# A hybrid attention / linear-attention layer: the low-rank gate projection taken from the scaled tokens, its shift added as a bias

## The chip, the cores and the metric

The kernel runs on one core of one Trainium2 chip. A core has five engines that run side by side, each with its own queue of instructions in order: TensorE (PE in the profile; its weight loads are listed apart as PEld), VectorE (DVE), ScalarE (ACT), GpSimd (POOL) and SyncE (SP), which here only issues transfers. Matrix products accumulate in PSUM, a small memory of banks of 128 partitions by 512 fp32 numbers; everything else lies in SBUF. The metric is the device time of one execution in microseconds (us); the kernel before took 1984.97 us as the median of three runs (1984.95 to 1985.31).

## The reference, cut to what matters

The layer works on 256 latent tokens and 256 context tokens of width 2048, in fp32. The change touches one small projection of it, the low rank of the decay gates of the linear attention (GLA):

```python
h  = rms_norm(x, g_mix) * (1 + scale) + shift          # scale, shift: one vector each for latent, one each for context
qa, ka, va, qb, kb, vb, rb, lrf, lrb, gate_a, gate_b = split(h @ w_in)
gf = log_sigmoid(lrf @ w_gate_f + b_gate_f) / 16       # lrf, lrb: 16 columns each of h @ w_in
gb = log_sigmoid(lrb @ w_gate_b + b_gate_b) / 16
```

`lrf` and `lrb` are together 32 of the 13344 columns of `w_in`. The scale and shift vectors come from a product of the conditioning vector with `w_mod` (2048 by 12288). All that follows (two token mixers, the merge, the feed-forward part) is untouched.

## The kernel before, in words

**Tiles.** Tokens are held transposed: 2048 features as 16 K tiles of 128 partitions, by 256 tokens. The input tokens stand in four buffers `xr0` to `xr3` (`xr0`, `xr1`: latent, K tiles 0 to 7 and 8 to 15; `xr2`, `xr3`: context), 8 KB in each partition. They are 4 of the 16 slots of the tag "M". The products with the large weights are made in a split form: an fp32 number is the sum of a rounded part (`hi`) and a rest (`lo`), both in the type fp32r, and a product is three passes, hi·hi, lo·hi, hi·lo. The split tokens `h00hi`, `h00lo`, ... (first digit latent or context, second digit the half of the K tiles) take 8 more M slots. Weights come in blocks of 512 KB (`raw`, 7 slots), and ACT and DVE split them into `whi` and `wlo` (L207, L208; 3 slots each). A plain fp32 product, without the split, appears in the trace as two records.

**The opening.** The scale and shift vectors are not there at the start, so the first stage goes through the 16 K tiles in five groups (0-1, 2-3, 4-7, 8-11, 12-15). For each group `mod_both` loads the columns of `w_mod` (tile `mraw`, 1 MB each, M slots), multiplies them on PE (`pm`, L95), turns the result (`mtr`, DVE L324) into columns (`pcol`, PE L95, then copies L334), and then `affine_scale` (L488) multiplies the tokens by scale and norm factor **in place in `xr`**, and `affine_shift` (L495, L496) adds the shift and writes `hi` and `lo`. With these the group's K tiles of four blocks of projections run: QB twice, KB, VB (`acc`, L83), added up over the groups in SBUF (L505). The modulation products of the next group are put between the projection's products (`tick`, `midway`, `mid`), so PE does them while the loads of the weights go on. Every load of this stage goes through `load`, which fixes their order on SP's queue; a load that waits for a slot holds up all behind it. In the groups up to 8-11 the order of PE's products is fixed by hand (`opening`, `pe_seq`); after that the scheduler of the language orders them by its own cost model, by position in the program first. A slot of a tag is given to the next tile when the last reader of the old one is done.

**The low rank.** After the last group (L656 to L680) the 32 columns of `w_in` are fetched by POOL's queue into `wlr` (pieces of 128 bytes), and 64 plain fp32 products make the low rank: for 4 K tiles at a time, for latent and context, for `hi` and for `lo`, four products into four quarters of 32 partitions of one bank `pl` (L665; tile name `plr` in the trace). ACT copies the bank to `lrp` (L670), four products with a selection matrix add the four quarters and spread the sum to all of them (L673), and ACT and DVE form the split left factor `lr` (tile `wgl`, L676, L679). Then `gla_A` starts: its first product is `pz` (L705, in the trace L95), which needs `lr`. Beside it, PE runs the second KB block (`kb_block`, L855), whose products are free of the low rank.

**PSUM.** `bank` gives out banks of two tags, "main" (1 bank) and "side" (3 banks). `pm` is a side bank; `pcol` is a main bank; so are `plr` and `plr2`. The tag "fb" has 4 buffers and holds, in this stage, `cS` (the conditioning vector, to the last modulation product), the `mtr`, `wlr` and `lrp`.

Of the kernel before, what the change touches and what calls it, by code (L numbers as in the profile page):

```python
# [8 lines left out]
F32 = mybir.dt.float32  # L9
F32R = mybir.dt.float32r  # L10
U8 = mybir.dt.uint8
AF = mybir.ActivationFunctionType
# [4 lines left out]
P = 128  # L17
D = 2048
T = 256
KT = D // P  # L20
# [5 lines left out]
LR, GA, GB = 9216, 9248, 11296  # L26
# [5 lines left out]
def layer_kernel(ctx, tc, A, out):  # L32
    nc = tc.nc
    V, S, G, PE = nc.vector, nc.scalar, nc.gpsimd, nc.tensor
# [12 lines left out]
    w_in = A["w_in"][0]  # L47
    F2_BUFS = {"fa": 4, "fb": 4, "fc": 6}

    def M(name, shape, dt=F32):  # L50
        return big.tile(shape, dt, name=name, tag="M")

    def W2(tag, name, shape, dt=F32):
        return f2.tile(shape, dt, name=name, tag=tag, bufs=F2_BUFS[tag])

    def bank(name, shape=(P, 512), side=False):

        return ps.tile(list(shape), F32, name=name, tag="side" if side else "main", bufs=3 if side else 1)
# [11 lines left out]
    last, pin = [None], [None]  # L70

    opening = []

    def pe_seq(i):

        if opening and opening[0] is not i.ins:
            in_order(opening[0], i.ins)
            opening[:] = [i.ins]
        return i
# [14 lines left out]
    def mm_b(*a, **k):  # L94
        return pe_seq(after(PE.matmul(*a, **k)))  # L95
# [6 lines left out]
    def load(dst, src):  # L102

        d = nc.sync.dma_start(dst, src).ins
        last_load[:] = [d]
        if chain and chain[-1] is None:
            chain[:] = [d]
        elif chain:
            tc.add_manual_dep(d, chain[-1].name, mybir.DependencyInfo(
                mybir.DependencyClass.NoSync, mybir.DependencyReason.DATA), reason="order of loads")  # L110
            chain[:] = [d]
        return d
# [8 lines left out]
    xr = [M(f"xr{i}", [P, 8, T]) for i in range(4)]  # L121
# [96 lines left out]
    def proj_nat(w, r0, c0, kts, lhs, evac, by_tile=False, mid=None):  # L218


        banks = [acc.tile([P, 512], F32, name="acc", tag="acc") for _ in lhs]
        mms = []
        for k0 in kts[::2]:
            tick()
            nk = min(2, kts[-1] + 1 - k0)
            hi, lo = wsplit(w[r0 + k0 * P:r0 + (k0 + nk) * P, c0:c0 + 512])

            def part0(i):
                for k in range(nk):
                    kt = k0 + k  # L230
                    ahi, alo = lhs[i](kt)
                    mm(banks[i], ahi, hi[:, k, :], start=(kt == kts[0]), stop=False)
                    mms.append(mm(banks[i], alo, hi[:, k, :], start=False, stop=False).ins)

            def part1(i):
                for k in range(nk):
                    kt = k0 + k
                    mms.append(mm(banks[i], lhs[i](kt)[0], lo[:, k, :], start=False,
                                         stop=(kt == kts[-1])).ins)

            if by_tile and k0 + nk > kts[-1]:
                for i in range(len(lhs)):
                    if i == len(lhs) // 2:
                        midway()
                    part0(i)
                    part1(i)
                    if i:
                        in_order(end, mms[-4])
                    end = mms[-1]
            else:  # L250
                for part in (part0, part1):
                    for i in range(len(lhs)):
                        part(i)
                    if part is part0:
                        (mid or midway)()
        for i in range(len(lhs)):
            evac(i, banks[i])
# [46 lines left out]
    ALL = list(range(KT))  # L304


    def mod_both(part, t0, n, dst, put=None):

        a = []
        w = n * P  # L310
        nk = 16 // n

        def step(k0):
            if k0 == 0:
                a.append(bank(f"pm{part}_{t0}", (P, w), side=True))
            raw = M("mraw", [P, nk, w])
            load(raw, A["w_mod01"][part, t0 + k0 // nk].rearrange("p (c d) -> p c d", c=nk))
            for k in range(nk):
                kt = k0 + k
                q = 32 * (kt % 4)  # L320
                mm_b(a[0][q:q + 32, :], cS[:, kt, :], raw[:, k, :], start=(kt < 4), stop=(kt >= 12))
            if k0 == KT - nk:
                tr = W2("fb", "mtr", [P, n, 4, 32])
                V.transpose(tr.rearrange("p a b c -> p (a b c)"), a[0])  # L324
                a.append(tr)
                if put is not None:
                    put(end)

        def end():
            pc = bank(f"pcol{part}_{t0}", (32, n * 4, 2))  # L330
            mm_b(pc, sel[:, 0:32], a[1].rearrange("p a b c -> p (a b) c")[:, :, 0:2], start=True, stop=True)
            pv = pc.rearrange("p (a b) c -> p b c a", b=4)
            for b4 in range(4):
                V.tensor_copy(dst[32 * b4:32 * b4 + 32, :, t0:t0 + n], pv[:, b4, :, :])  # L334
            b0 = part * 16 + t0
            d = dst[:, :, t0:t0 + n]
            V.tensor_tensor(d, d, bmod[:, b0:b0 + n].unsqueeze(1).to_broadcast([P, 2, n]), op=ALU.add)

        steps = [lambda k0=k0: step(k0) for k0 in range(0, KT, nk)]
        return steps if put is not None else steps + [end]  # L340
# [48 lines left out]
    shift1 = cst.tile([P, 2, KT], F32, name="shift1")  # L389
# [110 lines left out]
    def add_to(dst, first):  # L500
        def evac(i, b):
            if first:
                S.activation(dst(i), b, AF.Copy)
            else:
                V.tensor_tensor(dst(i), dst(i), b, op=ALU.add)  # L505
        return evac

    hh, hl = [[], []], [[], []]
# [34 lines left out]
    kts = ALL[0:2]  # L543
# [36 lines left out]
    hold.extend([None, i])  # L580
    hold_hi.extend([None, j])

    for gi, (t0, n) in enumerate(groups):
        if gi == 0:
            continue
        kts = ALL[t0:t0 + n]
        flush()
        while bg_steps:
            bg_steps.pop(0)()
        flush()  # L590
        mid = None
        if gi + 1 < len(groups):
            bg_steps.extend(mods[gi + 1][0] + mods[gi + 1][1])
            ticks = 4 * ((n + 1) // 2)
            bg_rate[:] = [1.4 * len(bg_steps) / ticks + 0.01, 0.0]
            if gi == 1:
                bg_rate[:] = [0.0, 0.0]
                steps = iter([1, 2, 1, 2, 2, 0])

                def mid():  # L600
                    pin[0] = last[0]
                    for _ in range(next(steps)):
                        bg_steps.pop(0)()
                    pin[0] = None
        if t0 == 8:
            more_h(1)
        for s in range(2):
            if gi > 1:
                affine_scale(s, t0, n)
                affine_shift(s, t0, n)  # L610
            if s == 0:
                for j in range(2):
                    if j and mid is not None:
                        mid()
                    proj_T(w_in, QB + j * 512, kts, [h_all(0)], add_to(lambda i, j=j: qb0[2 * j + i], False),
                           mid=mid if j else None)
                if mid is not None:
                    mid()
        proj_T(w_in, KB, kts, [h_all(0), h_all(1)], add_to(lambda i: kbt[:, i, :], False), mid=mid)
        if mid is not None:  # L620
            mid()
        proj_nat(w_in, 0, VB, kts, h_xc, add_to(lambda i: vb0[:, i, :], False), mid=mid)
        if gi > 2:
            opening.clear()

# [3 lines left out]
    gate = cst.tile([P, 2], F32, name="gate")  # L629
# [23 lines left out]
    V.tensor_tensor(wg[64:P, :], wtm[64:P, :], wg[64:P, :].bitcast(F32), op=ALU.subtract)  # L653


    wlr = W2("fb", "wlr", [P, KT, 32])  # L656
    G.dma_start(wlr, w_in[:, LR:LR + 32].rearrange("(k p) d -> p k d", p=P))
    behind_gate.__exit__(None, None, None)
    pl = bank("plr")
    for k4 in range(4):  # L660
        for s in range(2):
            for part in (hh, hl):
                for k in range(4):
                    kt = 4 * k4 + k
                    PE.matmul(pl[32 * k:32 * k + 32, s * T:(s + 1) * T], wlr[:, kt, :],  # L665
                              part[s][kt // 8][:, kt % 8, :].bitcast(F32),
                              start=(k4 == 0 and s == 0 and part is hh),
                              stop=(k4 == 3 and part is hl), skip_group_check=True)
    lrp = W2("fb", "lrp", [P, 512])
    S.activation(lrp, pl, AF.Copy)  # L670
    pl = bank("plr2")
    for j in range(4):
        PE.matmul(pl[32 * j:32 * j + 32, :], sel[:, 0:32], lrp, start=True, stop=True)  # L673
# [500 lines left out]
    for half, blocks in enumerate((range(0, 6), range(6, 11))):  # L1174
        n = len(blocks)
# [128 lines left out]
```

## Time and profile before

| | us |
|---|---|
| median of 3 runs | 1984.97 |
| the profiled execution's own time | 1985.05 |
| its span, first to last instruction | 1983.1 |
| PE busy in the span | 1958.6 |
| DVE busy | 1400.0 |
| ACT busy | 971.2 |
| the 64 low-rank products, from the first's start to the next product of PE | 201.43 to 208.47 |

The page of the profile lists busy times and groups of instructions; the view of stretches gives busy time, granted clock and DMA traffic of chosen windows; the timeline lists instructions in order of time, merged, with "start us, us, engine line op out<-in shapes xcount [idle before <-releaser]"; the view of waits sums the idle time of an engine by what ended it. Times in the timeline count from the start of the span. The duration of a PE record includes its way through the array, so what a product costs is read from the distance of starts.

### The profile page before, as it was taken

How to read it: one execution, taken by the hardware profiler on the slowest of the kernel's cores; microseconds unless marked ns; L12 is line 12 of the kernel's file. 1: busy time of each engine (PE TensorE's matmuls, PEld its weight loads, DVE VectorE, ACT ScalarE, POOL GpSimd, SP SyncE). 2: the span in 40 equal slices, each digit the busy share in tenths (PEclk: the TensorE clock that was granted, in tenths of full speed). 3: DMA queues.
4: the chain of work that ended last, by engine and by line, in shares of the span. 5: the costliest groups of instructions: out<-in, count | busy, mean ns of one | idle time of the engine just before them, and what ended most of it. 6: DMA issues, size and time to landing. Idle time of an engine off the chain costs nothing.

```text
span 1983.1 us, 27131 instructions
## 1 busy us (share of the span) xinstructions
PE 1958.6 (99%) x10324; PEld 1637.9 (83%) x10324; DVE 1400.0 (71%) x2150; ACT 971.2 (49%) x1413; POOL 44.5 (2%) x61
## 2 busy tenths in 40 slices
PE   7999999999999999999999999999999999999999
PEld 5679888888887788888888888888888888888887
DVE  5765667876858888777776457889887555677754
ACT  4323555553345666444444445755555334555532
POOL 0010010112000000000000000000000000000000
PEclk9999999999999999999999999999999999999999
DMA  9965222336753456888888668688886566666563
GB/s 379 413 262 178 65 85 75 107 98 196 249 156 112 127 181 210 267 289 287 295 281 272 232 224 282 193 271 278 259 275 232 192 193 190 190 190 184 190 215 113
DMA packets 183603, 420.90 MB, mean 212 GB/s; under 512 B 12544, under 2 KB 12768, under 8 KB 178736
## 3 DMA queue, kind: packets, MB, share of 16 engines
q1 hardware_dynamic: 181856, 413.19, 63.8%
q0 software_dynamic: 1440, 5.80, 1.0%
q8 instruction: 81, 1.33, 0.3%
q14 instruction: 50, 0.41, 0.1%
q10 hardware_dynamic: 176, 0.17, 0.0%
HBM read 416.98 MB, written 2.13 MB: 211 GB/s over the span
## 4 chain that ended last, share of the span: by engine, by line
PE 68%; DVE 0%; ACT 0%; issue 0%; DVEq 0%
PE acc L83 52%; PE accs L83 12%; PE poa L95 1%; PE pS L95 1%; PE ptp L98 1%; PE pto L98 0%; PE ptx L98 0%; DVE wlo L208 0%; ACT s L973 0%; PE ptq L98 0%; DVE s L978 0%; DVE yd L1225 0%; DVE yd L1219 0%; DVE raw L365 0%; ACT whi L207 0%
## 5 line engine op out<-in xcount | busy, mean ns | idle before, releaser
L208 DVE TENSOR_TENSOR wlo<-raw,whi 128x1024 fp32r<-128x1024 f32 x568 | 694.8, 1225 | 435.0 <-ACT whi L207 394.7
L207 ACT ACTIVATE whi<-raw 128x1024 fp32r<-128x1024 f32 x568 | 601.1, 1059 | 773.3 <-PE acc L83 619.4
L83 PE MATMUL accs<-h,whi 128*128 128x512 f32 x704 | 176.3, 392 | 0.0
L83 PE MATMUL acc<-h,whi 128*128 128x512 f32 x640 | 160.4, 392 | 0.0
L83 PEld LDWEIGHTS accs<-h,whi 128*128 128x128 f32 x704 | 126.6, 189 | 22.6
L83 PE MATMUL acc<-whi,h01hi 128*128 128x512 f32 x352 | 139.9, 398 | 0.0
L83 PE MATMUL acc<-whi,h00hi 128*128 128x512 f32 x352 | 139.0, 395 | 0.0
L83 PE MATMUL acc<-whi,h00lo 128*128 128x512 f32 x352 | 138.0, 392 | 0.0
L83 PE MATMUL acc<-whi,h01lo 128*128 128x512 f32 x352 | 137.9, 392 | 0.0
L83 PE MATMUL acc<-whi,al 128*128 128x512 f32 x352 | 137.0, 389 | 0.0
L83 PE MATMUL acc<-whi,ah 128*128 128x512 f32 x352 | 137.0, 389 | 0.0
L83 PEld LDWEIGHTS acc<-h,whi 128*128 128x128 f32 x640 | 115.1, 189 | 20.6
L83 PEld LDWEIGHTS accs<-h,wlo 128*128 128x128 f32 x704 | 96.0, 190 | 6.8
L83 PE MATMUL acc<-wlo,h01hi 128*128 128x512 f32 x352 | 98.7, 396 | 0.0
L83 PE MATMUL accs<-h,wlo 128*128 128x256 f32 x704 | 98.2, 282 | 0.0
L83 PE MATMUL acc<-wlo,h00hi 128*128 128x512 f32 x352 | 97.7, 394 | 0.0
L83 PE MATMUL acc<-wlo,ah 128*128 128x512 f32 x352 | 94.3, 389 | 0.0
L83 PEld LDWEIGHTS acc<-h,wlo 128*128 128x128 f32 x640 | 87.4, 190 | 6.3
L83 PE MATMUL acc<-h,wlo 128*128 128x256 f32 x640 | 89.4, 282 | 0.0
L365 DVE CUSTOM_DVE_ANT_0 raw<-raw,csrow,pack 128x1024 f32<-128x1024 f32 x64 | 81.7, 1284 | 0.0
L83 PEld LDWEIGHTS acc<-whi,ah 128*128 128x128 f32 x352 | 66.1, 188 | 13.7
L83 PEld LDWEIGHTS acc<-whi,al 128*128 128x128 f32 x352 | 66.1, 188 | 13.6
(389 smaller groups left out, 3566.0 us busy)
## 6 DMA issues: line engine op xcount, KB each, us to landing
raw<-in_w_in SPq DMA_DIRECT2D x208, 512.0 KB, 4.4
raw<-in_w_up SPq DMA_DIRECT2D x176, 512.0 KB, 3.9
raw<-in_w_modT SPq DMA_DIRECT2D x128, 512.0 KB, 4.6
raw<-in_w_down SPq DMA_DIRECT2D x88, 512.0 KB, 3.7
mraw<-in_w_mod SPq DMA_DIRECT2D x32, 1024.0 KB, 13.3
raw<-in_w_attn_o SPq DMA_DIRECT2D x32, 512.0 KB, 4.9
raw<-in_w_gla_o SPq DMA_DIRECT2D x32, 512.0 KB, 4.7
raw<-in_w_out SPq DMA_DIRECT2D x32, 512.0 KB, 4.8
```

What stands on the lines that cost most here:

```text
L83: r = pe_seq(PE.matmul(*a, **k))
L95: return pe_seq(after(PE.matmul(*a, **k)))
L98: return pe_seq(after(PE.transpose(*a)))
L207: j = S.activation(hi[:, 0:n, :], raw[:, 0:n, :], AF.Copy).ins
L208: i = V.tensor_tensor(lo[:, 0:n, :], raw[:, 0:n, :], hi[:, 0:n, :].bitcast(F32), op=ALU.subtract).ins
L365: i0 = V.tensor_tensor_reduce(out=raws[i], in0=raws[i], in1=row[0], scale=1.0, scalar=d if h else bmod[:, b0:b0 + 1], op0=ALU.mult, op1=AL ...
```

## The change

The low rank is made from the scaled tokens in `xr` before the shift is added. Since h = xs + shift, the low rank of h is that of xs plus the low rank of the shift, which is one number for each of the 32 columns, for latent and for context. So the products run over `xr` (fp32, one part in place of `hi` and `lo`): 32 in place of 64, eight K tiles at a time, in two runs; the first stands behind the VB products of the group 4-7, the second behind those of the group 12-15. Both add into one bank `pl`, of the tag main, which is held from the first run to the end of the second. `pcol` moves to the tag side. The shift's share is made by 16 products with two moving columns (latent, context) into a bank `plb`; ACT copies it to two columns (into the old tile `gate`) and adds them as a bias while it copies `pl` to `lrp`, in two instructions of 256 columns in place of one of 512. `wlr` is now loaded on SP's queue, in the fixed order of loads, behind the weights of the second group, from a host array `k_wlr` that holds the 32 columns with 2 KB in a row for each partition; the load on POOL's queue goes.

```diff
         def end():
-            pc = bank(f"pcol{part}_{t0}", (32, n * 4, 2))
+            pc = bank(f"pcol{part}_{t0}", (32, n * 4, 2), side=True)
...
     hold_hi.extend([None, j])
 
+    wlr = W2("fb", "wlr", [P, KT, 32])
+    load(wlr.rearrange("p k d -> p (k d)"), A["k_wlr"])
+    pl = bank("plr")
+
+    def low_rank(kts):
+        for k4 in kts[::4]:
+            for s in range(2):
+                for kt in range(k4, k4 + 4):
+                    q = 32 * (kt % 4)
+                    pe_seq(PE.matmul(pl[q:q + 32, s * T:(s + 1) * T], wlr[:, kt, :],
+                                     xr[2 * s + kt // 8][:, kt % 8, :], start=(k4 == 0 and s == 0),
+                                     stop=(k4 == 12), skip_group_check=True))
+
...
         proj_nat(w_in, 0, VB, kts, h_xc, add_to(lambda i: vb0[:, i, :], False), mid=mid)
+        if t0 == 4:
+            low_rank(range(0, 8))
+        if t0 == 12:
+            opening[:] = [last[0]]
+            low_rank(range(8, KT))
         if gi > 2:
             opening.clear()
...
-    wlr = W2("fb", "wlr", [P, KT, 32])
-    G.dma_start(wlr, w_in[:, LR:LR + 32].rearrange("(k p) d -> p k d", p=P))
     behind_gate.__exit__(None, None, None)
-    pl = bank("plr")
-    for k4 in range(4):
-        for s in range(2):
-            for part in (hh, hl):
-                for k in range(4):
-                    kt = 4 * k4 + k
-                    PE.matmul(pl[32 * k:32 * k + 32, s * T:(s + 1) * T], wlr[:, kt, :],
-                              part[s][kt // 8][:, kt % 8, :].bitcast(F32),
-                              start=(k4 == 0 and s == 0 and part is hh),
-                              stop=(k4 == 3 and part is hl), skip_group_check=True)
+    pb = bank("plb", (P, 2), side=True)
+    for kt in ALL:
+        q = 32 * (kt % 4)
+        PE.matmul(pb[q:q + 32, :], wlr[:, kt, :], shift1[:, :, kt], start=(kt < 4), stop=(kt >= 12))
+    pbs = gate
+    S.activation(pbs, pb, AF.Copy)
     lrp = W2("fb", "lrp", [P, 512])
-    S.activation(lrp, pl, AF.Copy)
+    for s in range(2):
+        S.activation(lrp[:, s * T:(s + 1) * T], pl[:, s * T:(s + 1) * T], AF.Identity, bias=pbs[:, s:s + 1])
```

More of the change, by code (lines that the diff above doesn't have):

```diff
@@ L1292 @@
     data["w_upT"] = data["w_up"][0, :, 0:512].T.reshape(4, P, 2, 1024).transpose(0, 2, 1, 3)
+    data["k_wlr"] = data["w_in"][0, :, LR:LR + 32].reshape(KT, P, 32).transpose(1, 0, 2).reshape(P, KT * 32)
     data.update(consts)
```

## The prediction

> **What bounds the kernel now.** I read the page first, then the stretches of the opening, then PE's waits, then the timeline around the low rank.
>
> ```profile
> span 1983.1 us, 27131 instructions
> PE 1958.6 (99%) x10324; PEld 1637.9 (83%) x10324; DVE 1400.0 (71%) x2150; ACT 971.2 (49%) x1413; POOL 44.5 (2%) x61
> PE 68%; DVE 0%; ACT 0%; issue 0%; DVEq 0%
> ```
>
> PE is busy 99% of the span, and the chain that ended last is PE's own work. A busy record alone does not prove a full engine, so the stretches follow: window, length, then busy time of PE, PEld, DVE, ACT and POOL, granted clock, DMA share, GB/s.
>
> ```profile
> 0.00:36.00 36.00, 26.96 (x190) 20.48 (x191) 19.62 (x41) 18.37 (x25) 1.38 (x6) 0.95 0.97 369
> 36.00:101.00 65.00, 61.28 (x478) 42.82 (x477) 44.74 (x103) 21.10 (x34) 0.00 (x0) 1.00 1.02 412
> 101.00:201.40 100.40, 99.49 (x686) 84.66 (x684) 58.60 (x99) 30.86 (x41) 7.34 (x13) 1.00 0.64 215
> 201.40:208.50 7.10, 7.10 (x130) 4.09 (x129) 2.39 (x4) 0.00 (x0) 0.00 (x0) 1.00 0.25 74
> 208.50:1983.10 1774.60, 1763.72 (x8851) 1485.86 (x8847) 1274.62 (x1907) 900.91 (x1314) 35.82 (x42) 1.00 0.63 202
> ```
>
> Up to 36 us PE is held by loads. From 36 to 101 the DMA engines are full (share 1.02, 412 GB/s) and PE is 94% busy (61.28 of 65). From 101 on PE hardly stops, and for the 7.1 us of the low rank it does nothing else. What PE waits for between 36 and 201.4 is all in four rows:
>
> ```profile
> PE pcol L95 <- DVE mtr L324: 2.6, 4, 0.8
> PE acc L83 <- DVE wlo L208: 1.1, 3, 0.6
> PE acc L83 <- ACT h10hi L495: 0.7, 1, 0.7
> PE acc L83 <- DVE h10lo L496: 0.2, 1, 0.2
> ```
>
> No row names a transfer. So a microsecond taken from PE behind 36 us should reach the end, as long as no new wait takes its place.
>
> **The change part by part.** The stage it shortens:
>
> ```profile
> 201.43 0.64 PE L665 MATMUL plr<-h00hi,wlr 128*32 128x256 f32 x8
> 201.88 0.61 PE L665 MATMUL plr<-h00lo,wlr 128*32 128x256 f32 x8
> 207.93 0.61 PE L665 MATMUL plr<-h11lo,wlr 128*32 128x256 f32 x8
> 208.47 0.39 PE L83 MATMUL acc<-h00hi,whi 128*128 128x256 f32 x1
> 208.61 0.60 ACT L670 ACTIVATE lrp<-plr 128x512 f32<-128x512 f32 x1 [7.82 <-PE plr L665]
> 209.38 1.07 PE L673 MATMUL plr<-lrp,pack 128*32 128x512 f32 x8
> 210.51 0.69 ACT L676 ACTIVATE wgl<-plr,pack 128x512 fp32r<-128x512 f32 x1 [1.30 <-PE plr L673]
> 211.23 1.52 DVE L679 SCALAR_TENSOR_TENSOR wgl<-plr,pack,wgl 32x512 fp32r<-32x512 f32 x2 [7.44 <-ACT wgl L676]
> 213.59 0.63 PE L95 MATMUL pz<-wgl 128*128 128x512 f32 x2
> ```
>
> Removed: 64 products in 16 rounds of four (eight records each). The first starts at 201.43, the next product of PE at 208.47: **-7.04 us**.
>
> Added, the two runs: 32 products of the same shape, eight rounds. From the first to the last of the 16 rounds is 207.93 - 201.43 = 6.50 over 15, so 0.433 a round: **+3.46 us**, half at the end of the group 4-7, half in the old place. The first run stands between VB products and a modulation product of its own shape, so it changes the array's shape no oftener than before.
>
> Added, the two-column products: 16, so 32 records, 128 by 32 weights, two moving columns. None so narrow is in the trace. Nearest rows:
>
> ```profile
> 203.18 0.13 PEld L665 LDWEIGHTS plr<-h00hi,wlr 128*32 128x32 f32 x4
> 209.38 0.16 PEld L673 LDWEIGHTS plr<-lrp,pack 128*32 128x32 f32 x8
> 41.57 0.20 PE L95 MATMUL pcol<-mtr,pack 128*32 128x16 f32 x1 [0.57 <-DVE mtr L324]
> 41.63 0.18 PE L95 MATMUL pcol<-mtr,pack 128*32 128x16 f32 x1
> ```
>
> Four loads into four column groups are over in 0.13, eight in 0.16; so 32 take 8 x 0.13 = 1.04 or 4 x 0.16 = 0.64. Two records with 16 columns into one column group start 0.06 apart, which makes 32 x 0.06 = 1.9. A gain is excluded: they are new work on a full engine. I take **+1.04**, since the products go round the four groups as in the first row; ends 0.64 and 1.9.
>
> Added on ACT, behind these products: the copy of two columns, and two copies of 256 columns for one of 512. A copy of 512 took 0.60 (208.61); the shortest ends are nothing and one more such copy, so the chain to `pz` grows by 0 to 0.6. What hides it is the KB block on PE. In the trace `lr` for the first direction is done at 211.23 + 1.52 = 212.75 and `pz` starts at 213.59, 0.84 of slack. A chain 0.6 longer just fits. **+0.1**, ends 0 and 0.6. Queued behind the longer wait on ACT are `whi` copies for later KB products, three slots of which were filled before.
>
> Moved: `wlr` goes onto SP's queue at about 34 us. At 412 GB/s its 256 KB take 0.62 us, and every later load lands so much later. A block of that stage:
>
> ```profile
> 81.63 1.06 ACT L207 ACTIVATE whi<-raw 128x1024 fp32r<-128x1024 f32 x1 [1.96 <-DMA raw<-in_w_in]
> wlr<-in_w_in POOLq DMA_DIRECT2D x1, 256.0 KB, 8.4
> ```
>
> ACT did wait for that block, PE (four rows above) for none: three slots of `whi` lie between. **0**, ends 0 and +0.62 if that cover is gone. The load taken from POOL's queue (256 KB in small pieces, 8.4 us) was waited for by nobody: `lrp` waited for PE. Its going is worth 0; what is behind it on POOL, the filling of `segs`, is needed only for the GLA. `pcol` as a third user of the side banks: 0, a bank of `pm` is free once `mtr` is turned, and the 2.6 us of waits for `mtr` stay.
>
> Held longer: `xr0` and `xr2`. Before, their last readers are the shifts of the group 4-7 near 80 us, and their two M slots go on. Now they are held until the first run is done. The boundary to the group 8-11, and SP's queue there:
>
> ```profile
> 113.58 1.71 ACT L495 ACTIVATE h01hi<-xr,shift 128x256 fp32r<-128x256 f32 x4 [9.65 <-DVE shift L337]
> 114.12 1.69 DVE L496 SCALAR_TENSOR_TENSOR h01lo<-xr,shift,h01hi 128x256 fp32r<-128x256 f32 x4 [0.58 <-ACT h01hi L495]
> 122.90 1.06 PE L95 MATMUL pm<-mraw,cS 128*32 128x512 f32 x8
> 123.39 1.88 DVE L505 TENSOR_TENSOR vb<-vb,acc 128x512 f32<-128x512 f32 x3
> 123.90 0.39 PE L83 MATMUL acc<-h01hi,whi 128*128 128x256 f32 x1
> 125.18 1.22 DVE L208 TENSOR_TENSOR wlo<-raw,whi 128x1024 fp32r<-128x1024 f32 x1
> ```
>
> ```profile
> 100.85 0.38 SPq L104 DMA_DIRECT2D raw<-in_w_in  x1
> 128.09 4.39 SPq L104 DMA_DIRECT2D mraw<-in_w_mod  x2
> 132.57 0.39 SPq L104 DMA_DIRECT2D raw<-in_w_in  x1
> 133.05 0.42 SPq L104 DMA_DIRECT2D mraw<-in_w_mod  x1
> 138.44 1.06 ACT L207 ACTIVATE whi<-raw 128x1024 fp32r<-128x1024 f32 x1 [11.27 <-DMA raw<-in_w_in]
> ```
>
> The M slots are all taken here: SP stands from 101 to 128 until a modulation product frees one. So I count: 16 slots, `xr` four, `kbt`, `vb0`, the first half of `h` four, leaves six in place of eight for `mraw` and the second half of `h`. At least `h01lo` then waits for the first run, which ends 1.73 behind 122.90, at 124.63. PE does a modulation product first (1.00, 122.90 to 123.90) and wants `h01hi` and `h01lo` from 125.63. DVE has the VB sums to 123.39 + 1.88 = 125.27; the first K tile of `h01lo` (1.69 for four) is there at 125.7, the second at 126.1, against a want at some 126.0. If the `wlo` of 125.18 goes first, 1.2 later. **+0.3**, ends 0 and 1.5. Behind that point the count is what it was, and SP's wait ends, as before, with the second modulation product.
>
> Sum: -7.04 + 3.46 + 1.04 + 0.1 + 0.3 = **-2.1 us**, against the profiled execution's own 1985.05: 1982.9. The median, 1984.97, lies 0.08 under that execution, so I say 1982.9. With all the cheap ends: -7.04 + 3.46 + 0.64 = -2.9, so 1982.1; with all dear ends -7.04 + 3.46 + 1.9 + 0.6 + 0.62 + 1.5 = +1.0, so 1986.1.
>
> **The rivals.**
>
> *No gain: the two-column products run load by load.* If a weight load does not go on beside a running product, each of the 32 records costs its load:
>
> ```profile
> L665 PEld LDWEIGHTS plr<-h00hi,wlr x16: 106/110/110, 201.4 to 203.2; 128*32 128x32 f32 x16
> ```
>
> 32 x 0.11 = 3.5 in place of 1.04, and the sum is +0.4: 1985.4. Against it: the low rank's records start 0.433 / 8 = 0.054 apart, half of one load, so loads to other column groups do go on beside products. For it: there each product lasts longer than its load, here it is nothing, and the price may be that of the load's latency. The Trainium skill, "TensorE: Matmul & The Clock Gate", in Part 3 on row and column tiling, says that a weight load overlaps products in flight only where the row group differs; here all use all rows, so by that rule the time would be this rival's. The trace speaks against the rule for column groups, as just shown.
>
> *Slower: two M slots short at the group 8-11.* If the scheduler gives the slots of the first freed `mraw` to `h11hi` and `h11lo` too, the load that went out at 128.09 waits two products longer, to 133.05, and the next ones wait for products that are themselves held up by weights queued behind these loads. There is no slack there: a weight block issued at 132.57 was waited for until 138.44 by ACT, which had stood for 11.27. So PE loses 133.05 - 128.09 = 5.0 once, and about as much again when the last `mraw`, and three blocks of weights behind it, wait for a product in the delayed part. 1982.9 + 10 = 1993. For it: SP's stand of 27 us. Against it: the slots come back at 124.6, before SP's old wait ends at 128.09. It decides if SP's wait ends later than the second modulation product of the group 8-11.
>
> *Faster than I say.* Two-column products at 0.64, no wait for `h01lo`, and a wait of the GLA behind it gone, since its chain starts closer to the end of the low rank and its products fall among others:
>
> ```profile
> 228.20 1.16 PE L95 MATMUL pa<-q,kb 128*128 128x128 f32 x8 [1.00 <-DVE q L755]
> ```
>
> -7.04 + 3.46 + 0.64 - 1.00 = -3.9: 1981.1, and a little more would count as faster. Against it: that wait is for DVE, whose work does not shrink.
>
> **How the numbers follow.** A change of 0.2% (4.0 us) is about what a measurement of this kernel can tell from none. My forecast, 1982.1 to 1984.3, has a chance of 0.55; no gain (1984.3 to 1988.9, the dear ends included) 0.21; the slower rival, over 1988.9, 0.13; the faster one, below 1981.0, 0.11. So faster 0.11, same 0.76, slower 0.13. The range takes in the dear ends and the lower half of the slower rival's way, and a little beyond the faster rival: 1980.4 to 1989.5.
>
> **What would show it.** Two runs of 16 products, each 1.7 us from first to last start, one near 123, one near 201; the two-column products in 0.6 to 1.9; `pz` behind the low rank's end by some 5 to 6 us with no gap on PE; SP's wait ending with the second modulation product of the group 8-11; `h01lo` written at 125 to 126 and not at 114. The prediction is wrong if PE's waits between 101 and 201 grow by more than 2 us (slots, or a weight block that comes late), if the two-column products take over 2 us, or if PE's order in the GLA comes out otherwise, since the scheduler is free there.

## The result, and the profile after

The changed kernel took 1981.78 us (median of 18 runs, 1981.26 to 1983.67), the kernel before, timed beside it, 1985.34 (18 runs, 1984.81 to 1987.11): a ratio of 0.9982, 95% interval 0.9976 to 0.9988, or 3.56 us less. That is just inside the 0.2% that counts as no change here, though the interval (2.4 to 4.8 us less) leaves out an unchanged time; and it is inside the range forecast, 1.1 us under the 1982.9. The profiled execution took 1981.30, with a span of 1979.5 (before: 1985.05 and 1983.1).

The view of stretches of the changed kernel, with the columns of the first fence of stretches:

```profile
36.00:101.00 65.00, 61.29 (x478) 42.83 (x478) 44.77 (x103) 20.97 (x34) 0.00 (x0) 1.00 1.02 411
101.00:201.40 100.40, 100.14 (x714) 85.15 (x713) 57.68 (x97) 30.64 (x41) 6.27 (x12) 1.00 0.64 215
```

From 36 to 101 us nothing moved (61.28 busy before, 61.29 now). From 101 to 201.4 PE is busy 100.14 of 100.40 us, before 99.49: 0.65 us of waiting went, which the forecast did not have. The view of PE's waits from 36 to 201.4 us says which:

```profile
PE pcol L95 <- DVE mtr L324: 2.6, 4, 0.8
PE acc L83 <- DVE wlo L208: 0.5, 2, 0.3
```

The wait for `wlo` fell from 1.1 to 0.5, and its one long piece, of 0.6, is gone. The timeline of the changed kernel, the two runs and what follows them:

```profile
122.78 1.93 PE L592 MATMUL plr<-xr,wlr 128*32 128x256 f32 x32
124.53 1.04 PE L95 MATMUL pm<-mraw,cS 128*32 128x512 f32 x8
202.25 1.93 PE L592 MATMUL plr<-xr,wlr 128*32 128x256 f32 x32
204.00 0.45 PE L678 MATMUL plb<-shift,wlr 128*32 128x2 f32 x32
204.38 0.39 PE L83 MATMUL acc<-h00hi,whi 128*128 128x256 f32 x1
204.60 0.17 ACT L680 ACTIVATE gate<-plb 128x2 f32<-128x2 f32 x1 [3.00 <-PE plb L678]
204.81 0.84 ACT L683 ACTIVATE lrp<-plr,gate 128x256 f32<-128x256 f32 x2
205.70 1.06 PE L686 MATMUL plr<-lrp,pack 128*32 128x512 f32 x8
207.56 1.52 DVE L692 SCALAR_TENSOR_TENSOR wgl<-plr,pack,wgl 32x512 fp32r<-32x512 f32 x2 [2.94 <-ACT wgl L689]
209.56 0.63 PE L95 MATMUL pz<-wgl 128*128 128x512 f32 x2
```

Each run takes 1.75 (124.53 - 122.78, 204.00 - 202.25). All 32 records of the two-column products take 0.38 (204.38 - 204.00). `pz` starts 5.18 behind the end of the low rank, before 5.12 (213.59 - 208.47), and the split left factor is done at 209.08, in time.

To see where time comes from, I compare the starts of the same products of PE in two timelines, both counted from the column product of the scale for the group 4-7 (62.26 us in the changed kernel), because executions of one kernel reach it at different times (last section). Against the kernel before, in us:

| kernel | first `h01hi` product, near 124 | column product near 137 | column product near 156 | end of the low rank | last product |
|---|---|---|---|---|---|
| the change | +1.72 | +0.95 | +0.94 | -3.97 | -4.01 |
| e1_hold | +0.09 | +0.10 | +0.09 | +0.09 | +0.14 |
| e2_hilo_two_runs | +3.45 | +2.56 | +2.03 | -1.43 | -1.40 |
| e4_dve_order | 0.00 | -0.39 | -0.40 | -0.40 | -0.39 |
| e9_two_behind | -0.01 | -0.81 | -0.84 | -0.84 | -0.86 |
| e3_pb4 | +1.71 | +0.94 | +0.91 | -3.18 | -3.25 |
| e5_late | -0.01 | 0.00 | +3.89 | +1.03 | +0.85 |
| e6_one_run | -0.01 | -0.01 | +3.94 | +1.03 | +0.88 |
| e7_gap | +1.72 | +1.34 | +1.31 | -3.60 | -3.74 |
| e8_wlr_sp | -0.02 | -0.02 | -0.05 | -0.05 | -0.16 |
| e10_true_gap | +0.86 | +0.48 | +0.48 | -4.43 | -4.53 |
| e11_gap_order | +0.86 | +0.07 | +0.06 | -4.85 | -5.03 |
| e13_lane7 | +0.86 | +0.08 | +0.07 | -4.84 | -4.80 |

Kernels with the same products up to the first column's place agree there within 0.02. At the last product differences under some 0.2 mean nothing: e8, in which no product was changed, stands at -0.16.

The first line holds three questions: why the second group of columns gives 0.77 back (+1.72 to +0.95), why the two-column products are so cheap, and where 0.4 us of the 4.0 on PE are lost, since span and median fell by 3.6 only.

### The profile page after: what moved, and what is told of

Same layout as the page of the kernel before. It is cut to its first block, busy times and chain, and to the rows that moved or that the text cites. A ratio compares the mean times of both kernels' runs of the same rounds, so it can differ in the third digit from the quotient of the medians.

```text
span 1979.5 us, 27075 instructions
## 1 busy us (share of the span) xinstructions
PE 1955.1 (99%) x10292; PEld 1636.0 (83%) x10292; DVE 1399.8 (71%) x2150; ACT 972.1 (49%) x1415; POOL 44.2 (2%) x60
## 3 DMA queue, kind: packets, MB, share of 16 engines
q8 instruction: 80, 1.31, 0.3%
## 4 chain that ended last, share of the span: by engine, by line
PE 68%; DVE 0%; ACT 0%; issue 0%; DVEq 0%
PE acc L83 52%; PE accs L83 12%; PE poa L95 1%; PE pS L95 1%; PE ptp L98 1%; PE pto L98 0%; PE ptx L98 0%; DVE wlo L208 0%; ACT s L986 0%; PE ptq L98 0%; DVE s L991 0%; DVE yd L1238 0%; DVE yd L1232 0%; DVE raw L365 0%; ACT whi L207 0%
```

## The experiments

**Does holding `xr0` and `xr2` cost anything?** e1_hold is the kernel before with two tiny products, which nobody reads, at the place of the first run.

```diff
+        if t0 == 4:
+            hb = bank("holdb", (32, 2), side=True)
+            for s in range(2):
+                pe_seq(PE.matmul(hb, sel[:, 0:32], xr[2 * s][:, 7, 0:2], start=(s == 0), stop=(s == 1)))
```

> The kernel before, with one addition: at the place of the first run, two products of two columns each read xr0 and xr2 into a bank that nobody reads, so that the two M slots are held as long as in the change and nothing else is done. Theory A (holding the slots costs nothing, and is not what took away PE's wait of 0.64 us for wlo at 135 us): time as before plus some 0.3 us for two small products, PE's waits for wlo 1.1 us as before, h11hi written behind 123 us. Theory B (the slots held change the order of loads and splits, and that took the wait away): the wait of 0.64 is gone, time 0.3 us under before. The slower rival of the prediction (two slots short): SP's wait from 101 us ends behind 130 us and the time grows by 5 to 10 us.

Ratio 1.0 (0.999 to 1.0009), and 0.09 on PE, the two products themselves. The wait for `wlo` is 1.2, before 1.1. `h11hi` did wait for the two products (it was written from 124.81 on), so the slots were held. Holding them to this place costs nothing, and it is not what removed the wait.

**The place and the length of the runs apart.** e2_hilo_two_runs keeps the two places, but with `hi` and `lo`, so the sum needs no bias.

```diff
-                for kt in range(k4, k4 + 4):
...
+                for part in (hh, hl):
+                    for kt in range(k4, k4 + 4):
...
-    pb = bank("plb", (P, 2), side=True)
...
```

> The changed kernel with the halving undone: 64 products over the hi and lo parts, in the two runs of the change, no two-column products and no bias; xr is not held. Products by the rows: 7.0 us in two runs of 3.5. Theory A (the halving is the gain, 3.46 us less 0.38 for the two-column products, and the place of the first run brings the rest by what it lets DVE do): 3.1 us over the changed kernel, and up to 0.9 under before. Theory B (the place of the runs brings nothing by itself): the time of before.

Ratio 0.9997 (0.9988 to 1.0007), PE 1.40 earlier at the end. The two runs together cost what the one block cost before (3.47 and 3.59), and 1.42 came back between them (+3.45 to +2.03). So the place alone brings a gain, more than I had said, and PE's row of waits for `wlo` falls from 1.1 to 0.2. The timeline of this kernel on DVE, and that of the kernel before, show how:

```profile
127.42 1.67 DVE L496 SCALAR_TENSOR_TENSOR h11lo<-xr,shift,h11hi 128x256 fp32r<-128x256 f32 x4 [1.14 <-issue]
135.19 1.22 DVE L208 TENSOR_TENSOR wlo<-raw,whi 128x1024 fp32r<-128x1024 f32 x1
```

```profile
130.66 1.29 DVE L505 TENSOR_TENSOR qb<-qb,acc 128x512 f32<-128x512 f32 x2 [4.25 <-PE acc L83]
131.86 0.88 DVE L496 SCALAR_TENSOR_TENSOR h11lo<-xr,shift,h11hi 128x256 fp32r<-128x256 f32 x2
133.66 0.84 DVE L496 SCALAR_TENSOR_TENSOR h11lo<-xr,shift,h11hi 128x256 fp32r<-128x256 f32 x2
134.41 1.22 DVE L208 TENSOR_TENSOR wlo<-raw,whi 128x1024 fp32r<-128x1024 f32 x1
135.69 1.21 PE L83 MATMUL acc<-h01hi,wlo 128*128 128x256 f32 x8 [0.64 <-DVE wlo L208]
```

Before, two pieces of `h11lo` stand directly ahead of the `wlo` that PE wants at 135.05 (135.69 - 0.64). In e2 all four are done at 129. In the changed kernel the scheduler put three ahead of the transpose `mtr`, none between it and `wlo`, and one behind:

```profile
132.26 1.29 DVE L505 TENSOR_TENSOR qb<-qb,acc 128x512 f32<-128x512 f32 x2 [5.98 <-PE acc L83]
133.46 1.27 DVE L496 SCALAR_TENSOR_TENSOR h11lo<-xr,shift,h11hi 128x256 fp32r<-128x256 f32 x3
134.65 0.71 DVE L324 STREAM_TRANSPOSE mtr<-pm 128x512 f32<-128x512 f32 x1
135.28 1.18 DVE L208 TENSOR_TENSOR wlo<-raw,whi 128x1024 fp32r<-128x1024 f32 x1
136.39 0.47 DVE L496 SCALAR_TENSOR_TENSOR h11lo<-xr,shift,h11hi 128x256 fp32r<-128x256 f32 x1
```

From the start of the `qb` sums, which a product of PE releases, to the start of that `wlo` are 3.75 us before (134.41 - 130.66) and 3.02 in the changed kernel (135.28 - 132.26).

**DVE's order alone.** e4_dve_order is the kernel before with one piece of `h11lo` (K tile 10) ordered behind `wlo`; e9_two_behind puts two there (10 and 11).

```diff
             i = V.scalar_tensor_tensor(lo, xk, sh, hi.bitcast(F32), op0=ALU.add, op1=ALU.subtract).ins
+            if s == 1 and kt == 10:
+                in_order(last_lo[0], i)
```

> The kernel before with one order added on DVE: the third h11lo of the group 8-11 (K tile 10) stands behind the wlo of the last QB block. Theory A (PE's wait of 0.64 us at 135 us was DVE's order: two h11lo stood ahead of that wlo): PE's waits for wlo fall from 1.1 to 0.5 us, the time by 0.4 to 0.7 us. Theory B (the wait went because the loads or PE's own time moved): the wait stays, no change.

> The kernel before with two h11lo of the group 8-11 (K tiles 10 and 11) ordered on DVE behind the wlo of the last QB block; one of them, in the run with one order, took 0.39 us off. If DVE's order is all of what the changed kernel gained there (0.77 us), PE's wait at 135 us is gone and PE is 0.6 to 0.8 us earlier behind it; if a part came from PE's own delay by the first run, no more than 0.4.

One piece gave 0.40 (ratio 1.0001, 0.9992 to 1.001), and the row of waits fell to 0.8 only, where 0.5 was expected; two gave 0.84 on PE (0.9997, 0.9988 to 1.0006). What the times can't tell, the starts do. The view of PE's waits of e9 has, with no other row longer than before:

```profile
PE acc L83 <- DVE wlo L208: 0.5, 2, 0.2
```

That is the changed kernel's total. From the `qb` sums to `wlo` are 3.36 us in e4 and 3.00 in e9, and in all 14 traces the row of waits goes with this stretch: 1.1 to 1.2 where it is about 3.75, 0.7 to 0.8 at 3.36 to 3.39, 0.5 at 3.00 to 3.02, and 0.2 in e2, where it is 1.20. Nothing of the low rank was touched in e4 and e9, so the 0.77 is the order on DVE, which a change of PE's program altered in passing.

**What a two-column product costs.** e3_pb4 is the changed kernel with these products made four times into the same bank, and a quarter of the sum taken.

```diff
+    for r in range(4):
-    for kt in ALL:
+        for kt in ALL:
...
-    S.activation(pbs, pb, AF.Copy)
+    S.activation(pbs, pb, AF.Copy, scale=0.25)
```

> The changed kernel with the 16 two-column products made four times and the sum scaled by a quarter in the copy. Theory A (32 records cost 0.38 us): 96 more records, 1.1 us more on PE between the second run and the KB block. The step of the prediction (1.04 us for 32): 3.1 us more. Load by load (0.11 us a record): 10.6 us more.

Ratio 0.9986 (0.9976 to 0.9995). The timeline of e3:

```profile
206.00 1.28 PE L679 MATMUL plb<-shift,wlr 128*32 128x2 f32 x128
207.21 0.38 PE L83 MATMUL acc<-h00hi,whi 128*128 128x256 f32 x1
```

128 records take 1.21, so 0.0095 each, and the table has the 96 more at 0.79 (-3.97 to -3.18), less than the 1.1 expected, since the records behind the first 32 cost less. They cost neither 0.033 a record (my 1.04) nor a whole load of 0.11 each.

**The slots.** e5_late moves the first run behind the group 8-11; e6_one_run makes one run of all 32 products at the end. Both hold `xr0` and `xr2` past the point that I had named as deciding.

```diff
-        if t0 == 4:
+        if t0 == 8:
             low_rank(range(0, 8))
```

```diff
-        if t0 == 4:
-            low_rank(range(0, 8))
...
-            low_rank(range(8, KT))
+            low_rank(ALL)
```

> The changed kernel with the first run one group later, behind the VB products of the group 8-11, so that xr0 and xr2 are held through that group. Slower rival of the prediction (two M slots short, SP's loads wait for later modulation products): SP's wait that began at 101 to 106 us ends behind 133 us in place of 129.7, ACT waits for weight blocks in the group 8-11, PE loses 5 to 10 us against the changed kernel. Against it, if slots are no limit: PE's time behind the low rank within 0.8 us of the changed kernel's (the wait of 0.64 us for wlo may come back).

> The changed kernel with one run of all 16 K tiles in the old place; xr0 and xr2 are held to the end of the opening. The products are the same, so if the place were without effect the time is the changed kernel's. Theory A (the place of the first run brought the wait of 0.64 us by DVE's order, and an early run frees two slots before they are wanted): the slots are missing in the group 8-11 and the loads behind them come 4 to 5 us late or more, so the time is that of before or over it; by the rival's sum 5 to 10 us over the changed kernel. Theory B (slots are no limit): 0.8 us over the changed kernel.

e5 took 1986.74 in one run, e6 1986.56 (ratio 1.0007, 0.9998 to 1.0016). SP's queue in e5 (timeline):

```profile
124.22 0.33 SPq L104 DMA_DIRECT2D mraw<-in_w_mod  x1
133.20 5.34 SPq L104 DMA_DIRECT2D mraw<-in_w_mod  x2
138.63 0.39 SPq L104 DMA_DIRECT2D raw<-in_w_in  x1
142.78 0.33 SPq L104 DMA_DIRECT2D mraw<-in_w_mod  x1
```

The load that goes out at 129.69 in the changed kernel waits to 133.20 here, the next to 138.63 and 142.78: the mechanism of my slower rival. PE pays in e6 as follows (timeline, then stretches):

```profile
144.16 1.06 PE L95 MATMUL pm<-mraw,cS 128*32 128x512 f32 x8 [0.32 <-DMA mraw<-in_w_mod]
147.09 0.39 PE L83 MATMUL acc<-h01hi,whi 128*128 128x256 f32 x1 [1.87 <-ACT whi L207]
148.40 0.42 PE L83 MATMUL acc<-h01lo,whi 128*128 128x256 f32 x1
148.62 0.41 PE L83 MATMUL acc<-h11hi,whi 128*128 128x256 f32 x1
```

```profile
144.00:148.00 4.00, 1.97 (x15) 1.06 (x16) 2.06 (x4) 1.06 (x1) 0.54 (x1) 1.00 0.98 352
148.00:152.00 4.00, 4.00 (x23) 4.00 (x22) 0.30 (x1) 0.65 (x1) 0.00 (x0) 0.57 1.01 398
```

It waits 0.32 + 1.87 = 2.2, and right behind it the granted clock is 0.57 over 4 us: the products start 0.22 apart (148.40, 148.62), elsewhere 0.12. Half the clock for (1 - 0.57) x 4 / 0.5 = 3.4 us costs 1.7, and 2.2 + 1.7 = 3.9 is the +3.94 of the table. It came once: the second loss that I had added did not come. So the rival's price was about 4, not 10. Against the changed kernel e6 is 5.0 later at the end of the low rank (+1.03 against -3.97), the low end of the 5 to 10 expected, since it also lacks the 0.8 of DVE's order.

**Filling a wait with the first run.** PE waits 0.84 us for `mtr` twice between 60 and 75 us, and the low rank of the K tiles 0 to 3 can be made by then. e7_gap issues these 8 products at the head of the group 4-7, which proved too late: the wait lies ahead of it.

```diff
+        if t0 == 4:
+            low_rank(range(0, 4))
         flush()
...
-            low_rank(range(0, 8))
+            low_rank(range(4, 8))
```

> The changed kernel with the first run cut in two: the K tiles 0 to 3 (two rounds, 0.87 us) stand ahead of the column products of the shift of the group 4-7, where PE waits 0.84 us for mtr at 72 us; the K tiles 4 to 7 stay. If that wait takes them in: PE 0.8 us earlier than in the changed kernel behind that point, waits for mtr 2.6 us down to 1.8. If they delay the column products instead: no change.

Ratio 0.9984 (0.9975 to 0.9993). The timeline of e7 shows the wait still there and the products 6 us behind it:

```profile
74.83 0.25 PE L95 MATMUL pcol<-mtr,pack 128*32 128x32 f32 x2 [0.84 <-DVE mtr L324]
80.67 1.07 PE L592 MATMUL plr<-xr,wlr 128*32 128x256 f32 x16
```

So e7 tested nothing of the idea. e10_true_gap puts the same products directly ahead of the column product; e11_gap_order adds the order of e9 to it.

```diff
         def end():
+            if part == 1 and t0 == 4:
+                low_rank(range(0, 4))
             pc = bank(f"pcol{part}_{t0}", (32, n * 4, 2), side=True)
```

> The changed kernel, but the low rank of the K tiles 0 to 3 (8 products, 16 records) now stands directly ahead of the column product of the scale for the group 4-7, where PE waited 0.84 us for mtr near 62 us in the changed kernel; the other 24 products stay where they were. Theory (PE's own order and waits are all that counts in the opening): the row of the wait for mtr falls from 2.6 to about 1.8 us, 16 records at 0.054 cost 0.86 there and fill it, the first run near 123 us falls from 1.75 to 0.87, and the last product of PE comes 0.84 earlier than in the changed kernel: a span near 1978.7, a time near 1981.0. Rival (what PE saves here it loses at the next wait for a block or a vector): the waits behind it grow by 0.8 and the time stays at 1981.8.

> The kernel with the 8 products in the wait for mtr, and beside it two of the four pieces of h11lo ordered behind wlo on DVE. Theory: the wait for wlo (0.5 us in the changed kernel, 2 times, longest 0.3) goes down to one of 0.26, so 0.2 to 0.3 on top of the 0.84: a span near 1978.4, a time near 1980.7. Rival (h11lo becomes late in its place): a wait for h11lo of 0.4 or more appears and the time is that of the kernel without the order, 1981.0, or more.

e10 took 1981.05 (ratio 0.998, 0.9972 to 0.9989), e11 1980.53 (0.9978, 0.9969 to 0.9988). The timeline of e10, then its view of PE's waits:

```profile
60.12 1.07 PE L95 MATMUL pm<-mraw,cS 128*32 128x512 f32 x8
61.00 1.05 PE L594 MATMUL plr<-xr,wlr 128*32 128x256 f32 x16
62.02 0.25 PE L95 MATMUL pcol<-mtr,pack 128*32 128x32 f32 x2
```

```profile
PE pcol L95 <- DVE mtr L324: 1.7, 3, 0.8
PE acc L83 <- DVE wlo L208: 0.8, 3, 0.3
```

From `pm` to the column product are 1.90, as in the changed kernel (60.35 to 62.26), so 16 records ride free, and +1.72 near 124 us becomes +0.86. But the wait for `wlo` grew to 0.8 again, which gave 0.4 back: so much was right in the rival. With two pieces of `h11lo` behind it (e11) the 0.4 came back too; its row of waits is 0.5, not the single 0.26 expected.

**The load of `wlr`, and the lost 0.4 us.** e8_wlr_sp is the kernel before with only the load moved to SP's queue.

```diff
+    load(wlr.rearrange("p k d -> p (k d)"), A["k_wlr"])
...
-    G.dma_start(wlr, w_in[:, LR:LR + 32].rearrange("(k p) d -> p k d", p=P))
```

> The kernel before, with only the load of wlr moved: onto SP's queue behind the weights of the second group, from the host array. Theory (the load is hidden): every product of PE between 62 us and the end starts within 0.1 us of the kernel before. Rival (the DMA engines are full there, and PE feels it): 0.62 us later from some block on, to the end.

Its one run took 1987.13 us and holds the half clock of the last section, so I go by the starts. PE's starts agree with the kernel before within 0.05 through the opening, and within 0.16 at the last product, a little over the 0.1 expected: the load is hidden. But the end is not the same. The last pair of PE's records before, then in the changed kernel, then in e8 (timelines; spans 1983.1, 1979.5 and 1985.0):

```profile
1978.15 0.61 PE L83 MATMUL acc<-wlo,ah 128*128 128x512 f32 x2
```

```profile
1974.02 0.61 PE L83 MATMUL acc<-wlo,ah 128*128 128x512 f32 x2
```

```profile
1979.58 0.61 PE L83 MATMUL acc<-wlo,ah 128*128 128x512 f32 x2
```

The spans are printed to 0.1; by the unrounded ends in the traces it is 5.00, 5.43 and 5.43 us from there to the end. In all the kernels with one load more on SP's queue it is 5.43 to 5.44, in the others 4.99 to 5.01 (the expectation below has wider bounds, worked out with the rounded spans). SP's semaphore instructions, which no view lists, are in the trace; counted from PE's last start:

```
before                            the change
2.36 to 2.73  seven waits         2.30  two waits done
3.88  the tenth wait (landing)    3.89  the third wait (landing)
3.95  SP's first drain            3.95, 4.01, ... 4.31  seven more waits, then 4.38 SP's first drain
```

At its end the program asks the semaphores of its transfers one by one, 0.06 us each; in the trace the transfers on SP take eight of them in turn. With one load more in front, the last output lands on the first of the eight in place of the last, and seven waits that were done beforehand come behind it: 7 x 0.062 = 0.43. e13_lane7 is e11 with seven loads of one number more, which nobody reads, so that the turn comes round again.

```diff
+    pad = sm.tile([KT, P], F32, name="pad", tag="t128", bufs=2)
+    for i in range(7):
+        d = nc.sync.dma_start(pad[0:1, i:i + 1], A["k_pack"][0:1, i:i + 1]).ins
+        in_order(last_load[0], d)
+        last_load[:] = [d]
```

> The kernel with the 8 products in the wait for mtr and with two pieces of h11lo behind wlo, and beside it seven loads of one number each on SP's queue, behind the loads of the opening (near 200 us), which nobody reads. Theory: the program's loads and stores take eight landing semaphores in turn, and at the end SP asks them one after the other, 0.06 us each. In the kernel before the last output lands on the eighth, in all kernels with one load more on SP on the first, so SP has seven more to ask behind the last landing: 7 x 0.06 = 0.43, which is the longer stretch from the last pair of PE's records to the end of the span (4.95 to 5.04 without wlr on SP, 5.39 to 5.48 with it). With seven loads more the last output is on the eighth again: the stretch falls from 5.39 to about 4.96 with PE's starts unmoved, and the time from 1980.5 to about 1980.1. Rival 1 (the longer stretch comes from the added input array or from POOL's missing load): it stays at 5.4 and the time at 1980.5. Rival 2 (the seven loads hold up the weights behind them): PE waits for whi or wlo between 200 and 215 us and the time grows by 0.5 or more.

1980.19 us (ratio 0.9974, 0.9964 to 0.9984), the fastest of all, 1.6 under the changed kernel. Its last pair of PE's records:

```profile
1974.93 0.61 PE L83 MATMUL acc<-wlo,ah 128*128 128x512 f32 x2
```

The span is 1979.93 unrounded, so 5.00 from there to the end, as in the kernel before; the last transfer is on the eighth semaphore again, and PE's waits near 200 us did not change. So the cause of the lost 0.4 is shown.

## Why the prediction was right, and where not

The forecast was no change that can be told, with 1982.9 us and -2.1 us against the kernel before. It came out at -3.56 (by the interval, -2.4 to -4.8, which leaves out -2.1): inside the range, but beyond the sum with all the cheap ends (-2.9, so 1982.1). 1981.78 lies in the strip from 1981.0 to 1982.1, to which the forecast had given no chance. By its terms:

| term | forecast | measured |
|---|---|---|
| 64 products out | -7.04 | -7.04 (in two runs, e2: 3.47 + 3.59) |
| two runs | +3.46 | +3.50 |
| two-column products | +1.04 (0.64 to 1.9) | +0.38 |
| chain from ACT to `pz` | +0.1 | 0 on PE (`pz` 0.06 later) |
| wait for `h01lo` | +0.3 (0 to 1.5) | 0 |
| load of `wlr` | 0 | 0 on PE |
| DVE's order at `wlo` | not seen | -0.77 |
| the closing waits of SP | not seen | +0.43 |
| sum | -2.1 | -3.5, against -3.56 |

That the sum is no further off is partly luck: of the two terms not seen, one took off what the other half put back.

*Right:* the stage is bound by PE's own work, so what left PE arrived. The runs came out at 1.75 each where 1.73 was said, and the load of `wlr` and the longer chain stayed hidden, as `pz` shows.

*Mis-sized:* the two-column products, even under the low end. The step that failed was to charge eight groups of four loads 0.13 each, one group behind the other. The 0.13 runs from the first load's start to the last one's end, so it holds the length of a load, 0.11, and the sum counted that length eight times. The second of the prediction's rows had the price of a further group: eight loads are over in 0.16, four in 0.13, so four more take 0.03, and 0.13 + 7 x 0.03 = 0.34 would have been near the 0.38 measured. The trace of the changed kernel has

```profile
203.79 0.58 PEld L678 LDWEIGHTS plb<-shift,wlr 128*32 128x32 f32 x32
```

32 loads in 0.58, where one behind the other they would take 3.5. This refutes the rival with no gain. It also speaks against the sentence of the Trainium skill behind it, "TensorE: Matmul & The Clock Gate", Part 3: the loads overlap although the row group is the same throughout.

*Wrong:* the wait for `h01lo`. I had counted the slots rightly, but gave the missing ones to the wrong tile. The timeline of the changed kernel:

```profile
113.46 1.71 ACT L495 ACTIVATE h01hi<-xr,shift 128x256 fp32r<-128x256 f32 x4 [9.66 <-DVE shift L337]
114.01 1.68 DVE L496 SCALAR_TENSOR_TENSOR h01lo<-xr,shift,h01hi 128x256 fp32r<-128x256 f32 x4 [0.58 <-ACT h01hi L495]
124.34 0.33 SPq L104 DMA_DIRECT2D mraw<-in_w_mod  x1
124.78 1.71 ACT L495 ACTIVATE h11hi<-xr,shift 128x256 fp32r<-128x256 f32 x4 [7.71 <-PE plr L592]
129.69 4.39 SPq L104 DMA_DIRECT2D mraw<-in_w_mod  x2
```

`h01hi` and `h01lo` were written at 113 to 114, as before. The context's half, `h11hi`, waited for the run (124.78), and SP, which waited for the run too, sent out a `mraw` behind it (124.34). PE needs `h11hi` first at 144.5, so nobody on its path waited. SP's next stand ends at 129.69, with the second modulation product, as said; e5 and e6 show what happens when it ends later.

*Not seen:* the order on DVE (e4, e9), and the closing waits (e8, e13), which I had not counted among the things that one more transfer on SP moves. I had said that a load moved past a queue costs what its bytes cost; it also shifted which semaphore the last store uses. The faster rival needed the wait for `q` in the GLA to go; it stayed (1.00 before, 0.9 after), and the gain beyond the forecast came from elsewhere.

## What to carry to other kernels

Where an engine is busy 99%, the distance of starts of the very instructions that go and come gives most of the answer. What is left is the order that a scheduler gives the *other* engines: ask which buffer is wanted next at each wait that exists already, and who stands in the queue ahead of its maker. To judge a change of 2 us in 2000, compare the starts of the same products in two traces from an anchor behind the noisy opening, and look at the tail behind the last product separately.

## What the runs showed of the hardware

**Narrow products into four column groups start 9 to 12 ns apart on average** (0.38 / 32, 1.21 / 128), each with its own load of 32 columns. The Trainium skill, "TensorE: Matmul & The Clock Gate", Part 1, puts the least distance of starts at about 25 ns however narrow the product; by that, as an estimate, 32 would take 0.8. The runs here disagree, for products that go round four column groups.

**A wait can cost nearly twice its length.** The window of e1_hold from 32 to 36 us, then that of e10:

```profile
32.00:36.00 4.00, 3.89 (x23) 3.89 (x24) 3.84 (x6) 3.69 (x7) 0.00 (x0) 0.69 1.01 422
```

```profile
32.00:36.00 4.00, 4.00 (x30) 3.78 (x30) 3.71 (x6) 3.98 (x7) 0.00 (x0) 1.00 1.02 424
```

In e1 PE had waited 1.88 us for `qb` at 32.1 and then ran at half clock for a while; in e10 it had waited 1.45 and did not. In every profiled execution with a wait of 1.73 to 2.14 there (e1, e3, e4, e6, e7, e8, e9, e13) the clock fell; the same 1.42 to 1.45 at 20 us was followed by half clock in some executions (the two kernels compared, e2, e5, e11) and not in others; what decides it is not shown. Where the clock fell at 20 us, PE lost little: the column product from which the table counts starts at 62.0 in e10, at 62.3 to 62.6 in these, and at 63.7 to 64.3 in the eight where it fell at 32. This difference fits the 1.7 us by which runs of one kernel differ (1984.8 to 1985.4 or 1986.6 to 1987.1 before), though only one run of each kernel has a trace. The same fall of the clock is what made the lost slots of e6 cost 3.9 for 2.2 of waiting. The stretch of 3.4 us agrees with the window of 3413 ns that the Trainium skill gives, "TensorE: Matmul & The Clock Gate", Part 1.
